# Another order of expert blocks and of their weight loads, and another place for the shared down products, in a two-layer transformer kernel

## The chip, the cores and the metric

The kernel runs on one core of a Trainium2 chip. The metric is the device time of one execution in microseconds (us); the median of several runs stands for a kernel. One more execution was profiled, and the rows below come from it.

The engines of the core have their own instruction streams and meet through semaphores. TensorE (PE in the rows) multiplies matrices into PSUM; its weight loads (PEld) run beside the products. VectorE (DVE) and ScalarE (ACT) work on tiles, GpSimd (POOL) here mostly gathers token rows, and SyncE (SP, or SPq for its queue) issues nearly all transfers from memory. Transfers that SyncE issues go out in its program order: when one has to wait for its buffer, all that stand behind it wait too.

## The reference, cut to what matters

One token sequence of 512 passes two blocks. The first has attention and then a mixture of experts, and that is where the change lies: 64 experts, 6 for each token, and a shared expert for all tokens.

```python
def moe_ffn(h, w_router, b_router, w_exp_gate, w_exp_up, w_exp_down, w_sh_gate, w_sh_up, w_sh_down):
    scores = jax.nn.sigmoid((xf @ w_router).astype(jnp.float32))
    ...
    def expert_block(xs):
        tok, g, e = xs
        xb = x_pad[tok]
        hb = jax.nn.silu(xb @ w_exp_gate[e]) * (xb @ w_exp_up[e])
        return (hb @ w_exp_down[e]) * g[:, None]
    ...
    routed = jax.ops.segment_sum(yb.reshape(n_rows, D), row_tok, num_segments=T + 1)[:T]
    shared = (jax.nn.silu(xf @ w_sh_gate) * (xf @ w_sh_up)) @ w_sh_down
    return (shared + routed).reshape(B, S, D)
```

The model width D is 1024 and an expert's inner width 256, all in float32. So an expert has a gate and an up matrix of 1024 x 256 and a down matrix of 256 x 1024, three MB in all.

## The kernel before

The work of the experts is cut into 32 blocks of 128 token slots. A block serves one, two or three experts: `KINDS` gives how many blocks there are of each kind and how the 128 slots are shared out. Two blocks are fixed to experts 0 to 3, 5 have one expert (128 slots), 5 have three (64, 32, 32), and the other 20 have two (96, 32 or 64, 64). Which expert falls to which place is found at run time, by how many tokens each has.

The list `seq` sets the order in which TensorE takes the blocks. For each block TensorE does, in program order: the gate and up products (`expert_h`, line 1009, on `raw`, `rawh`, `rawl` or `raws` weights), the transposes of the next block's tokens (line 994), the first half of the products that add the block before into the residual (`combine`, lines 1054 and 1055), the transpose of the hidden values (line 1019), the second half of `combine`, and the down products (`expert_out`, line 1033, on `whi`, `wlo` or `rawd` weights). After some blocks small products follow that work out the token slots of later blocks (`slot_info`, line 971).

The weights come by SyncE. A gate/up load is half of an expert's gate and up matrix, two transfers of 512 KB, and takes one place in a ring of buffers `gu` (3 `rawh`, 6 `raw`, 2 `rawl`, and, after the first round, the one buffer `raws`). A down load is half of a down matrix, one transfer of 512 KB, and takes one place in a ring of eight (3 `whi`, 3 `wlo`, 2 `rawd`). Before the loop, `phase_b` writes the list `stream` of all loads. Time is counted in half steps there: 2i is the gate/up of the i-th block of `seq`, 2i + 1 its down products. `free` is the half step that gives the load's buffer back. The list is sorted, and `issue(now)` takes loads from its head as long as their buffers are free at half step `now`.

The shared expert's down products are four chunks of 128 tokens, each of four 512-wide products that stand as two instructions each (line 1409, on `raws` and `hsT`). Their weights `wd` lie in the buffer `raws` from before the loop. `down_at` says after which block's gate/up a chunk comes: before, the chunks are in the blocks 0, 1, 2 and 3. `raws` joins the ring of `gu` when the fourth is done.

After the block before the last come a test for experts with more tokens than slots, the last block, and the second model block.

Of the kernel before, what the change touches and what calls it, by code (L numbers as in the profile page):

```python
# [17 lines left out]
OP = mybir.AluOpType  # L18
AX = mybir.AxisListType

T, D, NCH = 512, 1024, 4
# [37 lines left out]
class Kern:  # L59
# [861 lines left out]

    def gu(self, h):
        self.turn += 1
        n = self.NP + self.NX + self.NY
        t = self.turn if self.turn < n else (self.turn - n) % (n + 1)
        if t < self.NP:
            return self.hold.tile([128, self.RAW], F32, name="rawh", bufs=self.NP)
        if t < self.NP + self.NX:
            return self.raw(2048)
        return self.spare() if t < n else self.last()  # L930

    def last(self):
        return self.rp.tile([128, self.RAW], F32, name="raws")
# [124 lines left out]
    def phase_b(self):  # L1058
        nc, tc, I = self.nc, self.tc, self.I
        xr, hT, hp = self.xres, self.h2T, self.hp  # L1060
# [6 lines left out]
        wd = self.last().rearrange("p (k n) -> p k n", k=2)  # L1067
# [34 lines left out]
        hsT = rt.tile([128, 2, T], F32, name="hsT")  # L1102
# [11 lines left out]
        for j in range(3):  # L1114
            t = rt.tile([128, D], F32, name=f"xg{j}")
# [5 lines left out]
        p = 0  # L1121
# [75 lines left out]
        p = 0  # L1197
# [6 lines left out]
        for name, src in (("pos", pos), ("gate", sco)):  # L1204
            t = self.tps()
# [4 lines left out]
            t = self.tps()  # L1210
# [45 lines left out]
        def info(bs):  # L1256
            b0, b1 = bs[0], bs[-1] + 1
            return self.slot_info(ep, b1 - b0, [(x, y, slot[:, :, o * NB + b0:o * NB + b1], lambda c, j, o=o: pay[:, c, o * NB + b0 + j, :])
                                                for x, y, o in self.parts(b0)], (tok[:, b0:b1], tokf[:, b0:b1], gate[:, b0:b1]))
# [8 lines left out]
        ks = [list(range(p, p + n)) for p, n in zip(np.cumsum([0] + [k[0] for k in self.KINDS]).tolist(), [k[0] for k in self.KINDS])]  # L1268
        seq = ks[0][:]
        for i, p in enumerate(ks[2] + ks[3] + ks[5]):  # L1270
            seq.append(p)
            if i % 4 == 2:
                seq += [ks[4].pop(0), ks[1].pop(0)]
        assert sorted(seq) == list(range(NB))


# [1 line left out]
        n = 2  # L1278
        while todo:
            p = todo[0]  # L1280
# [4 lines left out]
            n = 3  # L1285

        stream, ngu, ndn = [], self.NP + self.NX + self.NY, self.NHI + self.NLO + self.ND
        ug, ud = [], []  # L1290
        for i, p in enumerate(seq):
            es = self.experts(p)
            for h in range(2):
                for j in es:
                    t = len(ug)
                    free = -1 if t < ngu else 2 * ug[t - ngu] if t < 2 * ngu else 7 if t == 2 * ngu else 2 * ug[t - ngu - 1]
                    ug.append(i)
                    if i >= STAT:
                        stream.append((free, 2 * i, len(stream), p, j, h))
            for j in es:  # L1300
                for k in range(2):
                    t = len(ud)
                    free = -1 if t < ndn else 2 * ud[t - ndn] + 1
                    ud.append(i)
                    if i >= STAT:
                        stream.append((free, 2 * i + 1, len(stream), p, j, 2 + k))
        last = {0: -1, 1: -1}
        for n, (free, *r) in enumerate(stream):
            last[r[-1] > 1] = free = max(free, last[r[-1] > 1])
            stream[n] = (free, *r)  # L1310
        stream.sort()
        ids_of = {}

        def issue(now):

            while stream and stream[0][0] <= now:
                _, _, _, p, j, h = stream.pop(0)
                if (p, j) not in ids_of:
                    ld, (e,) = nc.values_load_multi_w_load_instructions(
                        ids[0:1, j * NB + p:j * NB + p + 1], engines=[mybir.EngineType.SP], min_val=0, max_val=E - 1)  # L1320
                    if len(ends) > 2:
                        self.order(ends[-3], ld[0])
                    ids_of[p, j] = e
                e, w = ids_of[p, j], loads.setdefault(p, {}).setdefault(j, [None] * 4)
                if h < 2:
                    w[h] = self.load_gu(self.gu(h), dyn, e, h)
                else:
                    w[h] = self.load_down(self.down(h - 2), dyn, e, h - 2)
                    ends.append(self.last_load)

        down_at = {0: [0], 1: [1], 2: [2], 3: [3]}
        ends, done = [], []
        fixed_down(1, 1)
        issue(-1)
        for d in sorted(k for k in due if k < 0):
            for bs in due.pop(d):
# [38 lines left out]
        def up(xT, p):  # L1375
            parts = tiles(p)
            return parts, self.expert_h(parts, xT, gate[:, p:p + 1])
# [5 lines left out]
        for i, p in enumerate(seq):  # L1383
            infos = [info(bs) for bs in due.get(i, [])]
            for g in infos[:1]:
                next(g)
            if nxt is None:
                nxt = up(xT, p)
            (parts, hs), nxt = nxt, None
            if i == NB - 2:  # L1390
                self.combine(done)
                done = []
                self.chain = None
                overflow()
                self.chain = []
            issue(2 * i)
            if i + 3 < NB:
                q = seq[i + 3]
                self.gather(xgs[i % 3], tok[:, q:q + 1])
            if i + 1 < NB:  # L1400
                xT = self.slots_T(xgs[(i + 1) % 3])
                if i + 1 >= NB - 1:
                    nxt = up(xT, seq[i + 1])
            for c in down_at.get(i, []):
                for n in range(2):
                    pd = self.acc()
                    s = slice(n * 512, (n + 1) * 512)
                    for k in range(2):
                        self.pe(nc.tensor.matmul(pd, hsT[:, k, c * 128:(c + 1) * 128], wd[:, k, s], start=(k == 0), stop=(k == 1)))
                    nc.vector.tensor_tensor(xr[:, c, s], xr[:, c, s], pd, op=OP.add)  # L1410
            y = None
            if i == NB - 1:
                y = self.hold.tile([128, self.RAW], F32, name="rawh", bufs=self.NP).bitcast(F32R)
                y = Split(y[:, :D], y[:, D:])
            if done and i < NB - 1:
                self.combine(done, range(0, 2))
            hT = self.hidden_T(hs)
            if done and i < NB - 1:
                self.combine(done, range(2, NCH))
                done = []  # L1420
            done.append((self.pick(tokf[:, p:p + 1]), self.expert_out(parts, hT, y)))
            for g in infos:
                self.run(g)
            issue(2 * i + 1)
        self.chain = None
        assert not stream
# [687 lines left out]
```

## Time and profile before

| what | value |
|---|---|
| median of three timed runs | 1771.95 us (1765.51 to 1772.01) |
| the profiled execution's own time | 1765.15 us |
| its span, first to last instruction | 1763.4 us |
| TensorE busy in the span | 1690.5 us (96%) |
| VectorE, ScalarE, GpSimd busy | 976.9, 581.4 and 69.0 us |
| mean granted clock of TensorE | 0.985 of full speed |
| moved by transfers | 341.90 MB, 194 GB/s on the mean over the span |

The expert blocks take the time from about 504 to 1052 us of the span. "Busy" says that an instruction was under way, not that it ran at full speed. The rows count idle time of an engine only ahead of an instruction, with what ended it. The granted clock is a share of 2.4 GHz: 1.00 is that level, 0.50 the level of 1.2 GHz, and a number between them a mixture over the stretch.

### The profile page before, as it was taken

What the parts mean: (1) busy time and instruction counts of PE and PEld (TensorE: products, weight loads), DVE (VectorE), ACT (ScalarE), POOL (GpSimd) and SP (SyncE); (2) the same over time, 40 slices, a digit from 0 to 9 for tenths busy, and PEclk for the clock granted to TensorE, in tenths of its full rate; (3) what the DMA queues carried; (4) which work ended last, traced back from release to release, by engine and by line L of the source; (5) the groups of instructions that cost most, each with busy time, mean ns of one, the idle gap of its engine ahead of it and who ended that gap; (6) DMA issues with size and microseconds to landing.
All of it is one profiled execution on the core that took longest, in us unless ns stands there. A gap on an engine that the chain in (4) does not pass through costs nothing. (4 is left out here: it accounts for less than half of the span.)

```text
span 1763.4 us, 23536 instructions
## 1 busy us (share of the span) xinstructions
PE 1690.5 (96%) x8740; PEld 1130.1 (64%) x8743; DVE 976.9 (55%) x1910; ACT 581.4 (33%) x1112; POOL 69.0 (4%) x107
## 2 busy tenths in 40 slices
PE   7899999999899999899999988999998999999999
PEld 2677766787654444354535437767866788888887
DVE  5585656366846665456546548655455744224422
ACT  3565444423111111111111123454557443114311
POOL 0000000000310000000000010000000000000000
PEclk9999999999999999999999998999999999999999
DMA  9233426138768999999999933201200432233230
GB/s 306 79 121 97 135 96 209 46 114 322 292 264 307 387 408 406 403 403 403 403 396 400 376 135 94 91 19 60 73 24 25 144 96 96 96 96 96 96 119 24
DMA packets 137895, 341.90 MB, mean 194 GB/s; under 512 B 12986, under 2 KB 59389, under 8 KB 137775
## 3 DMA queue, kind: packets, MB, share of 16 engines
q1 hardware_dynamic: 133168, 327.76, 50.7%
q0 software_dynamic: 4608, 12.59, 1.9%
q8 instruction: 71, 1.16, 0.3%
q14 instruction: 48, 0.39, 0.1%
HBM read 340.26 MB, written 4.21 MB: 195 GB/s over the span
## 5 line engine op out<-in xcount | busy, mean ns | idle before, releaser
L89 DVE TENSOR_TENSOR wlo<-raw,whi 128x1024 fp32r<-128x1024 f32 (+4 forms) x162 | 189.6, 1172 | 251.2 <-ACT whi L88 249.6
L88 ACT ACTIVATE whi<-raw 128x1024 fp32r<-128x1024 f32 (+4 forms) x162 | 164.4, 1019 | 253.3 <-PE acc L123 159.9
L1056 DVE TENSOR_TENSOR xres<-xres,acc 128x512 f32<-128x512 f32 x248 | 151.3, 682 | 0.5 <-PE acc L1055 0.5
L1009 PE MATMUL acc<-raw,xT 128*32 128x512 f32 (+2 forms) x704 | 140.2, 602 | 0.0
L121 PE MATMUL acc<-m_hh,whi 128*128 128x512 f32 (+1 forms) x272 | 103.4, 382 | 2.0 <-ACT m_hh L88 2.0
L1054 PE MATMUL acc<-yh,S 128*128 128x512 f32 x248 | 104.5, 421 | 0.0
L123 PE MATMUL acc<-m_hh,wlo 128*128 128x512 f32 (+1 forms) x272 | 103.7, 382 | 0.0
L122 PE MATMUL acc<-m_hl,whi 128*128 128x512 f32 (+1 forms) x272 | 103.7, 382 | 0.0
L88 ACT ACTIVATE yh<-yg 128x512 fp32r<-128x512 f32 x62 | 39.1, 630 | 194.8 <-DVE yg L1035 194.8
L123 PE MATMUL acc<-whi,ul 128*128 128x512 f32 x256 | 101.1, 395 | 0.0
L122 PE MATMUL acc<-wlo,uh 128*128 128x512 f32 x256 | 101.1, 395 | 0.0
L121 PE MATMUL acc<-whi,uh 128*128 128x512 f32 x256 | 101.1, 395 | 0.0
L1033 PE MATMUL acc<-wlo,hT 128*32 128x512 f32 (+2 forms) x312 | 98.9, 642 | 1.1 <-ACT hT L1021 1.1
L1009 PEld LDWEIGHTS acc<-raw,xT 128*32 128x32 f32 (+2 forms) x704 | 48.8, 131 | 79.5 <-issue 72.2
L1012 DVE SCALAR_TENSOR_TENSOR hs<-hs,gate,acc 128x256 f32<-128x256 f32 x32 | 15.4, 480 | 150.1 <-ACT hs L1011 150.1
L1055 PE MATMUL acc<-yl,S 128*128 128x512 f32 x248 | 97.5, 393 | 0.0
L1033 PE MATMUL acc<-whi,hT 128*32 128x512 f32 (+2 forms) x256 | 76.2, 628 | 13.9 <-DMA whi<-in_w_exp_down_dram 12.8
L121 PE MATMUL acc<-hh,whi 128*128 128x512 f32 x192 | 80.9, 421 | 0.0
L123 PE MATMUL acc<-hh,wlo 128*128 128x512 f32 x192 | 76.9, 401 | 0.0
L122 PE MATMUL acc<-hl,whi 128*128 128x512 f32 x192 | 76.9, 400 | 0.0
L1011 ACT ACTIVATE hs<-acc 128x256 f32<-128x256 f32 x32 | 12.3, 384 | 176.8 <-PE acc L1009 176.8
L286 DVE TENSOR_REDUCE st<-s 128x1 f32<-128x128 f32 (+1 forms) x96 | 46.5, 486 | 36.2 <-PE s L324 20.5
(612 smaller groups left out, 3548.3 us busy)
## 6 DMA issues: line engine op xcount, KB each, us to landing
raw<-in_w_exp_gate_dram SPq DMA_DIRECT2D x66, 512.0 KB
raw<-in_w_exp_up_dram SPq DMA_DIRECT2D x66, 512.0 KB
whi<-in_w_exp_down_dram SPq DMA_DIRECT2D x48, 512.0 KB
wlo<-in_w_exp_down_dram SPq DMA_DIRECT2D x48, 512.0 KB
raw<-in_w_in_dram SPq DMA_DIRECT2D x21, 1024.0 KB
rawh<-in_w_exp_gate_dram SPq DMA_DIRECT2D x33, 512.0 KB
rawh<-in_w_exp_up_dram SPq DMA_DIRECT2D x33, 512.0 KB
raw<-in_w_mod_dram SPq DMA_DIRECT2D x16, 1024.0 KB
```

The costliest lines, as they stand in the source:

```text
L88: self.nc.scalar.activation(hi, src, AF.Copy)
L89: return self.nc.vector.tensor_tensor(lo, src, hi.bitcast(F32), op=OP.subtract)
L121: mm(out, lh, rh, start=start, stop=False)
L122: mm(out, lh, rl, start=False, stop=False)
L123: mm(out, ll, rh, start=False, stop=stop)
L286: nc.vector.tensor_reduce(st[:, 1:2], s_ps[:, :n], axis=AX.X, op=OP.max, negate=True)
L1009: self.pe(nc.tensor.matmul(pg[a:b].rearrange("p (u n) -> p u n", u=2), xT[:, kk, a:b], ws[kk // 4][:, kk % 4], start=(kk == 0), stop=(kk = ...
L1012: nc.vector.scalar_tensor_tensor(hs, hs, gate, pg[:, 256:], op0=OP.mult, op1=OP.mult)
L1033: self.pe(nc.tensor.matmul(p[a:b], hT[:, j, a:b], ws[2 + j][:, s], start=(j == 0), stop=(j == 1)))
L1054: self.pe(nc.tensor.matmul(p, l, y.hi[:, s], start=(i == 0), stop=False))
L1055: self.pe(nc.tensor.matmul(p, l, y.lo[:, s], start=False, stop=(i == len(done) - 1)))
L1056: nc.vector.tensor_tensor(xr[:, c, s], xr[:, c, s], p, op=OP.add)
```

## The change

Three things change in the code. First, `seq`: before, after the third, seventh, eleventh, fifteenth and nineteenth of the two-expert blocks come a block of three and then one of one; now, after the third, fifth, seventh, ninth and eleventh, a block of one and then one of three. Written with F for a fixed block, 1, 2 and 3 for blocks of one, two and three experts:

```
before  F F 2 2 2 3 1 2 2 2 2 3 1 2 2 2 2 3 1 2 2 2 2 3 1 2 2 2 2 3 1 2
after   F F 2 2 2 1 3 2 2 1 3 2 2 1 3 2 2 1 3 2 2 1 3 2 2 2 2 2 2 2 2 2
```

Second, `stream` is sorted by the half step at which a load is wanted less 4 (`2 * i - 4` for gate/up, `2 * i - 3` for down), or by `free` where that is later, and no longer by `free` alone. A load at the head still waits until its buffer is free, and the others behind it wait with it. Third, the four chunks of shared down products go into the first four blocks of three, behind `combine` and right ahead of the down products; the buffer `raws` stays with them until then and never joins the ring of `gu`, which has 11 places throughout.

```diff
--- before.py
+++ after.py
@@ -921,13 +921,12 @@
     def gu(self, h):
         self.turn += 1
-        n = self.NP + self.NX + self.NY
-        t = self.turn if self.turn < n else (self.turn - n) % (n + 1)
+        t = self.turn % (self.NP + self.NX + self.NY)
         if t < self.NP:
             return self.hold.tile([128, self.RAW], F32, name="rawh", bufs=self.NP)
         if t < self.NP + self.NX:
             return self.raw(2048)
-        return self.spare() if t < n else self.last()
+        return self.spare()
     def last(self):
         return self.rp.tile([128, self.RAW], F32, name="raws")
@@ -1269,8 +1268,8 @@
         seq = ks[0][:]
         for i, p in enumerate(ks[2] + ks[3] + ks[5]):
             seq.append(p)
-            if i % 4 == 2:
-                seq += [ks[4].pop(0), ks[1].pop(0)]
+            if i % 2 == 0 and 2 <= i <= 10:
+                seq += [ks[1].pop(0), ks[4].pop(0)]
         assert sorted(seq) == list(range(NB))
@@ -1286,6 +1285,7 @@
         stream, ngu, ndn = [], self.NP + self.NX + self.NY, self.NHI + self.NLO + self.ND
         ug, ud = [], []
         for i, p in enumerate(seq):
@@ -1293,28 +1293,28 @@
             for h in range(2):
                 for j in es:
                     t = len(ug)
-                    free = -1 if t < ngu else 2 * ug[t - ngu] if t < 2 * ngu else 7 if t == 2 * ngu else 2 * ug[t - ngu - 1]
+                    free = -1 if t < ngu else 2 * ug[t - ngu]
                     ug.append(i)
                     if i >= STAT:
-                        stream.append((free, 2 * i, len(stream), p, j, h))
+                        stream.append((max(free, 2 * i - 4), free, 2 * i, len(stream), p, j, h))
             for j in es:
                 for k in range(2):
                     t = len(ud)
                     free = -1 if t < ndn else 2 * ud[t - ndn] + 1
                     ud.append(i)
                     if i >= STAT:
-                        stream.append((free, 2 * i + 1, len(stream), p, j, 2 + k))
+                        stream.append((max(free, 2 * i - 3), free, 2 * i + 1, len(stream), p, j, 2 + k))
         last = {0: -1, 1: -1}
-        for n, (free, *r) in enumerate(stream):
-            last[r[-1] > 1] = free = max(free, last[r[-1] > 1])
-            stream[n] = (free, *r)
+        for n, (at, *r) in enumerate(stream):
+            last[r[-1] > 1] = at = max(at, last[r[-1] > 1])
+            stream[n] = (at, *r)
         stream.sort()
         ids_of = {}
         def issue(now):
-            while stream and stream[0][0] <= now:
-                _, _, _, p, j, h = stream.pop(0)
+            while stream and stream[0][1] <= now:
+                p, j, h = stream.pop(0)[-3:]
                 if (p, j) not in ids_of:
                     ld, (e,) = nc.values_load_multi_w_load_instructions(
                         ids[0:1, j * NB + p:j * NB + p + 1], engines=[mybir.EngineType.SP], min_val=0, max_val=E - 1)
@@ -1328,7 +1328,8 @@
                     w[h] = self.load_down(self.down(h - 2), dyn, e, h - 2)
                     ends.append(self.last_load)
-        down_at = {0: [0], 1: [1], 2: [2], 3: [3]}
+        down_at = {i: [c] for c, i in enumerate([i for i, p in enumerate(seq) if len(self.experts(p)) == 3][:NCH])}
         ends, done = [], []
         fixed_down(1, 1)
         issue(-1)
@@ -1401,13 +1402,6 @@
                 xT = self.slots_T(xgs[(i + 1) % 3])
                 if i + 1 >= NB - 1:
                     nxt = up(xT, seq[i + 1])
-            for c in down_at.get(i, []):
-                for n in range(2):
-                    pd = self.acc()
-                    s = slice(n * 512, (n + 1) * 512)
-                    for k in range(2):
-                        self.pe(nc.tensor.matmul(pd, hsT[:, k, c * 128:(c + 1) * 128], wd[:, k, s], start=(k == 0), stop=(k == 1)))
-                    nc.vector.tensor_tensor(xr[:, c, s], xr[:, c, s], pd, op=OP.add)
             y = None
             if i == NB - 1:
                 y = self.hold.tile([128, self.RAW], F32, name="rawh", bufs=self.NP).bitcast(F32R)
@@ -1418,6 +1412,13 @@
             if done and i < NB - 1:
                 self.combine(done, range(2, NCH))
                 done = []
+            for c in down_at.get(i, []):
+                for n in range(2):
+                    pd = self.acc()
+                    s = slice(n * 512, (n + 1) * 512)
+                    for k in range(2):
+                        self.pe(nc.tensor.matmul(pd, hsT[:, k, c * 128:(c + 1) * 128], wd[:, k, s], start=(k == 0), stop=(k == 1)))
+                    nc.vector.tensor_tensor(xr[:, c, s], xr[:, c, s], pd, op=OP.add)
             done.append((self.pick(tokf[:, p:p + 1]), self.expert_out(parts, hT, y)))
             for g in infos:
                 self.run(g)
```

On SyncE, around the loads of the first block of three (blocks 5 and 7 before; 6 and 7 now). The names carry buffer numbers here: `whi_5117` and `whi_5119` are the two down loads of its third expert before, the `raw` loads the gate/up of the block two places further on. Before:

```order
L954 DMA rawd_4946<-in_w_exp_down_dram 128x1024
...
L954 DMA rawd_4948<-in_w_exp_down_dram 128x1024
...
L950 DMA raw_5012<-in_w_exp_gate_dram 128x1024
...
L950 DMA raw_5025<-in_w_exp_gate_dram 128x1024
...
L950 DMA raw_5028<-in_w_exp_gate_dram 128x1024
...
L950 DMA raw_5031<-in_w_exp_gate_dram 128x1024
...
L954 DMA whi_5117<-in_w_exp_down_dram 128x1024
...
L954 DMA whi_5119<-in_w_exp_down_dram 128x1024
```

Now, with `rawd_4932` the first expert's first down load, `whi_5039` and the two rows behind it the rest, and `raw_5055` the first gate/up load of the next block:

```order
L953 DMA rawd_4932<-in_w_exp_down_dram 128x1024
...
L953 DMA rawd_4934<-in_w_exp_down_dram 128x1024
...
L953 DMA whi_5037<-in_w_exp_down_dram 128x1024
...
L953 DMA whi_5039<-in_w_exp_down_dram 128x1024
...
L953 DMA whi_5041<-in_w_exp_down_dram 128x1024
...
L953 DMA wlo_5043<-in_w_exp_down_dram 128x1024
...
L949 DMA raw_5055<-in_w_exp_gate_dram 128x1024
```

The six down loads of the block of three now stand together and ahead of the next block's gate/up loads; before, the last two stood behind four gate/up loads of a later block.

On TensorE, around the first chunk of shared down products. Before, in block 0, between the transposes for the next block and the hidden values' transpose (block 0 has nothing to combine):

```order
L994 MATMUL t<-ident,xg_3745 128x128 x8
L1409 MATMUL acc<-raws,hsT 128x512 x4
L1019 MATMUL ht<-ident,hs 128x128 x2
L1033 MATMUL acc<-whi,hT 32x512 x7
L1033 MATMUL acc<-wlo,hT 32x512
```

Now, in block 6, between the last products of `combine` (1053 and 1054 are the lines 1054 and 1055 of before) and the down products (line 1033 before):

```order
L1053 MATMUL acc<-yh,S 128x512
L1054 MATMUL acc<-yl,S 128x512
L1420 MATMUL acc<-raws,hsT 128x512 x4
L1032 MATMUL acc<-rawd,hT 32x512 x2
L1032 MATMUL acc<-whi,hT 32x512 x2
```

The chunk has left block 0 and stands in front of the down products of the first block of three.

## Rows read from the trace of the kernel before

**Rows 1.** The page: its head, and busy time (us, share, instructions).

```profile
span 1763.4 us, 23536 instructions
...
PE 1690.5 (96%) x8740; PEld 1130.1 (64%) x8743; DVE 976.9 (55%) x1910; ACT 581.4 (33%) x1112; POOL 69.0 (4%) x107
```

**Rows 2.** Timeline, PE, blocks 0 and 30: start us, us, instruction.

```profile
503.97 1.05 PE L1009 MATMUL acc<-rawh,xT 128*32 128x512 f32 x2 [0.33 <-ACT xT L999]
...
1016.31 7.13 PE L1009 MATMUL acc<-raw,xT 128*128 128x512 f32 x16
```

**Rows 3.** Windows: length, busy by engine, granted clock, DMA share, GB/s.

```profile
540.00:560.00 20.00, 20.00 (x170) 10.15 (x166) 12.68 (x26) 2.63 (x5) 0.99 (x1) 1.00 0.82 317
560.00:574.00 14.00, 14.00 (x111) 5.67 (x104) 7.17 (x18) 2.24 (x4) 1.98 (x2) 1.00 0.62 212
600.00:1000.00 400.00, 387.17 (x2134) 185.89 (x2130) 230.62 (x430) 62.50 (x119) 22.82 (x23) 0.98 1.02 403
900.00:1000.00 100.00, 96.36 (x474) 45.20 (x470) 54.51 (x96) 15.65 (x30) 4.96 (x5) 0.97 1.02 399
712.00:720.00 8.00, 6.59 (x27) 1.59 (x28) 1.59 (x3) 0.63 (x1) 0.00 (x0) 0.57 1.02 399
```

**Rows 4.** Timeline, PE, an undisturbed block of two experts and the next start.

```profile
766.99 3.60 PE L1009 MATMUL acc<-rawh,xT 128*64 128x512 f32 x16
770.42 3.60 PE L1009 MATMUL acc<-raw,xT 128*64 128x512 f32 x16
...
779.05 0.64 PE L1033 MATMUL acc<-wlo,hT 128*64 128x512 f32 x1
...
782.53 7.04 PE L1009 MATMUL acc<-raw,xT 128*64 128x512 f32 x32
```

**Rows 5.** DMA view, 503 to 1017 us: total, the gathers' queue (packets, MB).

```profile
DMA packets 55724, 199.53 MB, mean 388 GB/s; under 512 B 7108, under 2 KB 7108, under 8 KB 55681
...
q0 software_dynamic: 4320, 11.92, 6.1%
...
xg<-h2d,tok POOLq DMA_INDIRECT x30, 7.4
```

**Rows 6.** Waits of PE, 503 to 1017 us: total us, times, longest.

```profile
PE acc L1033 <- DMA whi<-in_w_exp_down_dram: 12.8, 5, 6.0
```

**Rows 7.** Timeline, PE, down products of the second block of three.

```profile
706.34 0.62 PE L1033 MATMUL acc<-wlo,hT 128*32 128x512 f32 x2
...
713.41 1.06 PE L1033 MATMUL acc<-whi,hT 128*32 128x512 f32 x1 [6.01 <-DMA whi<-in_w_exp_down_dram]
```

**Rows 8.** Windows of line 1033 alone, undisturbed and five times disturbed.

```profile
778.00:784.00 6.00, 3.65 (x16) 1.00 1.03 405
608.00:616.00 8.00, 4.89 (x32) 1.00 1.03 408
705.00:720.00 15.00, 7.40 (x32) 0.77 1.02 404
809.00:820.00 11.00, 6.50 (x32) 0.84 1.02 401
909.00:922.00 13.00, 7.18 (x32) 0.74 1.02 399
1010.00:1017.00 7.00, 4.68 (x32) 1.00 0.31 112
```

**Rows 9.** Timeline, PE, a chunk of the shared down products.

```profile
550.52 3.60 PE L1409 MATMUL acc<-raws,hsT 128*128 128x512 f32 x8
```

**Rows 10.** Timeline, SP's queue, around raws and a late down load.

```profile
562.53 0.33 SPq L954 DMA_DIRECT2D wlo<-in_w_exp_down_dram  x1
573.63 0.34 SPq L950 DMA_DIRECT2D raws<-in_w_exp_gate_dram  x1
...
690.46 0.33 SPq L950 DMA_DIRECT2D raw<-in_w_exp_gate_dram  x1
...
701.97 0.33 SPq L954 DMA_DIRECT2D whi<-in_w_exp_down_dram  x1
```

## The prediction

> **What bounds the kernel now.** I read the page first: a span of 1763.4 us with TensorE busy for 96% of it [rows 1]. That share hides what the change touches, so the next view is the stretches of the expert stage, from the first gate/up product of block 0 at 503.97 us to that of block 30 at 1016.31 us [rows 2]: 512.3 us. Read the last two columns of [rows 3]: from 600 to 1000 us the DMA engines run at a share of 1.02 and 403 GB/s, full all the time, but from 540 to 560 us they move 317 GB/s and from 560 to 574 us only 212. So inside one stage the transfers idle early and are the limit later.
>
> How near is TensorE to a limit of its own? One undisturbed block of two experts takes 782.53 - 766.99 = 15.54 us from gate/up to gate/up; its down products begin 12.06 us after its start and take 3.5 us [rows 4]. A two-expert block needs 12 transfers of 512 KB, 6.29 MB, plus its gathered tokens (a share of 11.92 MB over 30 gathers, 0.40 MB) [rows 5]: 6.69 MB / 403 GB/s = 16.6 us. The engine needs 15.5 us a block, the weights 16.6: nearly balanced, and slightly in favour of the engine waiting.
>
> Where it waits is in one place. The table of waits gives 12.8 us, five times, longest 6.0, for down products on a down weight [rows 6]. The timeline shows the longest: the products start at 706.34 us, stop, and resume at 713.41 us [rows 7]. And they resume slower: 1.06 us for a product that took 0.62 just before, the granted clock over 712 to 720 us being 0.57, a mixture of the 2.4 GHz level and the 1.2 GHz one, after the engine stood still for 6 us [rows 3, 7]. To price the slow part I compare the busy time of the down products in five stretches with an undisturbed one [rows 8]: 4.89 + 7.40 + 6.50 + 7.18 + 4.68 = 30.65 us against 5 x 3.65 = 18.25, so 12.4 us more. Waits and their slow aftermath cost 12.8 + 12.4 = **25.2 us**. All five are blocks of three experts. Without them the stage would take 512.3 - 25.2 = **487.1 us**. A cross-check: 30 x 15.54 = 466.2, plus four shared chunks of about 3.5 (3.60 with the pipeline's end) [rows 9] = 14.0, leaves 7 us for the slot products between blocks, which is plausible.
>
> **The change, part by part.**
>
> *Order of the loads.* Take the second block of three. Eight gate/up transfers of a block further on are issued from 690.46 us on, and only then, at 701.97 us, the third expert's down weights [rows 10]; two transfers later they are used at 713.41, some 10 us after their issue. They were wanted at 706.34. The new list puts all six down loads of a block of three ahead of the next block's gate/up. And with a block of one expert in front, the ring of eight makes the third expert's loads wait for down buffers of the block two places before, not, as now, of the block just before. That gives 15.5 us more, against a lateness of 7 at most (713.41 - 706.34). I cost the removal at -25.2 us, the whole of the waits, since the lead grows by more than twice the worst wait.
>
> *Shared down products.* 32 matmuls (4 chunks) leave blocks 0 to 3 and enter the first four blocks of three. TensorE's work is the same: 0 us by itself, as matmuls do not vanish. What moves is time: blocks 0 to 3 end 3.5 us sooner each, so buffers come free sooner while transfers have room (317 and 212 GB/s), and in a block of three the 3.5 us lie ahead of the down products and give the weights that much longer. On VectorE two additions a chunk go along; it is not full, 230.6 us busy of 400 [rows 3]. I take 0.
>
> *One buffer less.* The shared weights stay in the buffer "raws" until the fourth block of three, so the ring has 11 places, not 12. This also takes a wait off the load queue: after 562.53 us nothing is issued until 573.63 us, when the first load into "raws" goes, right when chunk 3 releases it; everything behind it waits for 11 us, and this is the 212 GB/s stretch [rows 3, 10]. Price: a twelfth of the read-ahead, about a quarter of a block (4 us of lead). That cover is spent where the transfers are full anyway; bound it between 0 and the lead, 4 us once. I take 0.
>
> *A new wait.* Ordering by need puts down loads, which wait for buffers, ahead of gate/up loads whose buffers are already free. Queued behind a waiting down load on SyncE are the gate/up loads of the next block, and TensorE waits for those. At the start it means that block 3's gate/up is issued only after block 0's down products. It is wanted two blocks later, 31 us, and some eight transfers of 1.3 us (0.524 MB / 403 GB/s) are ahead of it, 10 us: hidden. What the new order can cost is idle transfer time.
>
> *The ledger of transfers.* From 503 to 1017 us 199.53 MB moved [rows 5]. Not wanted before block 30's second half of gate/up are block 30's down weights and all of block 31, 16 transfers, 8.4 MB. The other 191.1 MB at 403 GB/s need 474 us: done at 503 + 474 = 977 us if never idle. TensorE would want the last at 504 + 487 + 3.5 = 994.5. So 17 us of idle transfer time may be lost before the weights, not TensorE, set the end. Before, the loss was 20 x (403 - 317)/403 = 4.3 and 14 x (403 - 212)/403 = 6.6 us, 11 together [rows 3]. I expect about 6 (the wait for raws is gone, the new wait comes), so a margin of 11. At the rate of the lowest 100 us, 399 GB/s [rows 3], 5 us of it go; at 390 GB/s, 16 us, and it is overdrawn by 5.
>
> A rule that speaks against the change is weighed here. The row says 403 GB/s, held for 400 us [rows 3]. The Trainium skill (DMA: Bandwidth & Descriptors, Specifications) gives a limit of about 358 GB/s from memory for one core; by it the same bytes would take 534 us, and the stage would be longer than now. The trace disagrees with that figure where one core is at work, and the sum goes by the row.
>
> *Sum.* The profiled execution took 1765.15 us, 1.75 more than its span [rows 1]. 1765.15 - 25.2 = 1740.0. I add 1 us for a small wait that I can't see: **1741 us**. The three timed runs had a median of 1771.95, 6.8 above the profiled one, which is near the fastest of them (1765.51); the changed kernel may have such a spread too, and the range takes it in.
>
> **The rivals.**
>
> 1. *Part of it comes back.* The block after each block of three gets its second expert's down weights only when the three-expert block has released theirs, 12.06 us before use. A load into a full queue took some 10 us [rows 10], and two are needed (1.3 each): about 12.6, late by 0.5, and by 2 or 3 where the queue runs as slowly as in those rows ((701.97 - 690.46) / 8 = 1.44 us a transfer, not 1.3); a long stop would add the slow clock, (7.40 + 7.18 - 7.30) / 2 = 3.6 us [rows 8]. Five times 2 to 3 is 10 to 15 lost: 1750 to 1756. Against it: the six gate/up transfers just in front can be issued when the three-expert block's gate/up products end, 8.5 us sooner, so that the queue need not be full.
>
> 2. *Transfers were the limit anyway.* If the new waits leave them idle for 42 us in place of 11, the margin of 17 is overdrawn by 25 and the waits only change places: 1765. For it: the balance of 15.5 to 16.6 us a block, and a list that holds ready loads behind waiting ones. Against it: the first four blocks turn over faster, and the 11 us of room lie there.
>
> 3. *Slower.* Same place as rival 1, one price higher: if those six gate/up transfers are held as well, by a down load in front that waits, the second expert's weights stand behind 6 + 8 transfers, 14 x 1.3 = 18, and land 9 us late with 3.6 us of slow clock: 12.6 x 5 = 63, less 25.2: 1803. It decides from 5.0 us lost per block of three.
>
> 4. *The sustained rate falls.* With TensorE never stopping, the transfers have no more time in which to catch up. The time stays as it is if 191.1 MB fill the 516.8 us from 503 to 1019.8 (block 30's start now, and 3.5): 370 GB/s; 5% less than that, 352, is 26 us slower, 1791. Against it: no full 100 us have less than 399 [rows 3]. The Trainium skill's figure named above would give 503 + 534 - 1019.8 = 17 us more, 1782.
>
> **How the numbers follow.** Forecast (waits gone, 1735 to 1747): 0.75. Rival 1 (to 1757): 0.15. Rival 2: 0.06. Rival 3: 0.03. Rival 4: 0.01. The range 1735 to 1757 us leaves out little over 1 in 10 of these, and holds 8 in 10 with the runs' own spread. Half a percent, 8.8 us, is about what a measurement of this kernel can tell from no change. Faster by more than that: 0.75 + 0.15 = 0.90; within it 0.06; slower 0.04.
>
> **What would show it.** In the changed profile the waits of down products on down weights should fall from 12.8 us to under 2, the clock over 600 to 1000 us should read 1.00 and not 0.98, the stretch from first gate/up to block 30's should be 485 to 490 us, blocks 0 to 3 should be 3.5 us shorter, and the transfers should run above 390 GB/s from about 520 us on. Wrong would be: a wait on down weights in the block after each block of three (rival 1 or 3), on gate/up weights near the end (rival 2), or the same stage length with transfers full from 520 us on.

## The result, and the profile after

The changed kernel takes 1744.73 us (median of 4 runs, 1743.85 to 1748.16) against 1771.38 us of the kernel before in the same measurement (4 runs, 1765.51 to 1772.01). The ratio is 0.986, with a 95% interval of 0.9836 to 0.9885. The forecast was 1741 us, in a range of 1735 to 1757. A second measurement of the same two kernels (e9 below, 6 and 11 runs) gave 1747.5 against 1767.44 us, a ratio of 0.9882 (0.9862 to 0.9902). So the gain is 26.7 us in one measurement and 19.9 in the other.

The profiled execution took 1743.85 us. Its page, the span and the busy time by engine:

```profile
span 1741.8 us, 23494 instructions
...
PE 1680.4 (96%) x8742; PEld 1128.4 (65%) x8743; DVE 976.6 (56%) x1910; ACT 580.9 (33%) x1112; POOL 68.9 (4%) x107
```

TensorE's share, 96%, is that of [rows 1]: it says nothing of the change. The timeline of TensorE does, at the first gate/up products of blocks 0, 4 and 30 (helpers' line numbers are one less than before):

```profile
503.78 1.04 PE L1008 MATMUL acc<-rawh,xT 128*32 128x512 f32 x2 [0.33 <-ACT xT L998]
...
567.07 1.90 PE L1008 MATMUL acc<-raw,xT 128*32 128x512 f32 x16
...
991.24 0.59 PE L1008 MATMUL acc<-rawl,xT 128*64 128x512 f32 x1
```

The stage is 991.24 - 503.78 = 487.5 us, against 512.3 in [rows 2]: 24.9 us shorter. The forecast had 487.1. Blocks 0 to 3 take 63.3 us together; before, block 4 starts at 581.78 us, so they took 77.8: 14.5 us, or 3.6 a block, have left them. They come back as the chunks in the blocks of three.

The table of TensorE's waits from 500 to 1000 us answers to [rows 6]. It holds two rows, neither of them on a transfer:

```profile
PE acc L1032 <- ACT hT L1020: 0.5, 1, 0.5
PE acc L1008 <- ACT xT L998: 0.3, 1, 0.3
```

The windows answer to [rows 3]; the third column from the end is the granted clock, then DMA share and GB/s:

```profile
504.00:520.00 16.00, 15.53 (x158) 6.93 (x160) 8.22 (x21) 2.62 (x5) 1.97 (x2) 1.00 0.92 351
520.00:540.00 20.00, 20.00 (x174) 9.12 (x170) 13.54 (x33) 2.63 (x5) 1.98 (x2) 1.00 0.98 386
540.00:560.00 20.00, 20.00 (x188) 10.46 (x181) 11.04 (x26) 3.60 (x7) 0.98 (x1) 1.00 1.02 408
560.00:574.00 14.00, 14.00 (x113) 5.60 (x112) 8.39 (x14) 1.64 (x3) 0.99 (x1) 1.00 0.80 302
600.00:1000.00 400.00, 400.00 (x2260) 191.25 (x2249) 238.78 (x442) 63.97 (x122) 21.75 (x22) 1.00 1.02 403
900.00:1000.00 100.00, 100.00 (x486) 47.63 (x483) 56.83 (x104) 16.12 (x31) 3.96 (x4) 1.00 1.02 405
```

From 600 to 1000 us TensorE is busy for all of the 400 us at a clock of 1.00 (before: 387.17 and 0.98), and the transfers keep their 403 GB/s beside it. The forecast of more than 390 GB/s from about 520 us on is missed in two stretches: 520 to 540 us with 386, and above all 560 to 574 us with 302. SyncE's queue says why for the second:

```profile
555.42 0.33 SPq L949 DMA_DIRECT2D rawl<-in_w_exp_up_dram  x1
566.44 1.19 SPq L953 DMA_DIRECT2D wlo<-in_w_exp_down_dram  x2
```

The wait of 11 us for `raws` [rows 10] is gone, but a wait as long stands in its place: a down load at the head of the list, whose buffer block 3 gives back with its down products. Nobody on TensorE waits for it here.

The span is only 21.6 us shorter, though the stage gained 24.9. Where the other 3.3 us went is the last group of experiments.

### The profile page after: what moved, and what is told of

Its sections match the earlier page's. It is cut to its first block, busy times and chain, and to the rows that moved or that the text cites. A ratio compares the mean times of both kernels' runs of the same rounds, so it can differ in the third digit from the quotient of the medians.

```text
span 1741.8 us, 23494 instructions
## 1 busy us (share of the span) xinstructions
PE 1680.4 (96%) x8742; PEld 1128.4 (65%) x8743; DVE 976.6 (56%) x1910; ACT 580.9 (33%) x1112; POOL 68.9 (4%) x107
## 5 line engine op out<-in xcount | busy, mean ns | idle before, releaser
L1008 PE MATMUL acc<-raw,xT 128*32 128x512 f32 (+2 forms) x760 | 146.6, 598 | 0.0
L1032 PE MATMUL acc<-wlo,hT 128*32 128x512 f32 (+2 forms) x272 | 91.1, 596 | 0.9 <-ACT hT L1020 0.9
L1008 PE MATMUL acc<-rawh,xT 128*32 128x512 f32 (+2 forms) x408 | 83.1, 594 | 0.3 <-ACT xT L998 0.3
L286 DVE TENSOR_REDUCE st<-s 128x1 f32<-128x128 f32 (+1 forms) x96 | 46.4, 485 | 36.3 <-PE s L324 20.5
```

The lines of the kernel that those rows point to most:

```text
L286: nc.vector.tensor_reduce(st[:, 1:2], s_ps[:, :n], axis=AX.X, op=OP.max, negate=True)
L1008: self.pe(nc.tensor.matmul(pg[a:b].rearrange("p (u n) -> p u n", u=2), xT[:, kk, a:b], ws[kk // 4][:, kk % 4], start=(kk == 0), stop=(kk = ...
L1032: self.pe(nc.tensor.matmul(p[a:b], hT[:, j, a:b], ws[2 + j][:, s], start=(j == 0), stop=(j == 1)))
```

## The experiments

**Theory A**: the gain comes from transfer time that is no longer lost in the first blocks (the wait for `raws`, and four chunks during which full buffers stop the transfers). **Theory B**: it comes from the order of blocks and loads alone, as the prediction's sum put it. Total times of one kernel spread by up to 13 us, and part of that arises behind the expert blocks, in work that the change doesn't touch: from block 30's start to the span's end the profiles of e1 and e2 take 758.0 and 751.1 us. So beside the totals (medians, with the ratio to runs of before on the same chip) I compare the stage (block 0's to block 30's first gate/up) in each profile. Each kernel of the table has one profile, but for the changed one, whose two (the second is e9's) give the same 487.5 us. A place is a block's number in `seq`, counted from 0. "Lost" is the transfer time lost from 504 to 600 us, (403 - GB/s) / 403 x 96.

| kernel | total, us | ratio to before (95%) | stage, us | GB/s 504 to 600 | lost, us | TensorE's wait on transfers, us |
|---|---|---|---|---|---|---|
| before (profiled) | 1765.15 | | 512.3 | 348 | 13.1 | 12.8 |
| sort of loads only | 1764.36 | 0.9981 (0.9965 to 0.9996) | 503.5 | 343 | 14.3 | 8.7 |
| order of blocks only | 1773.36 | 1.003 (1.0012 to 1.0047) | 514.1 | 320 | 19.8 | 17.4 |
| sort and block order | 1757.89 | 0.9948 (0.9927 to 0.9969) | 500.5 | 317 | 20.5 | 6.9 |
| ring of eleven only | 1759.75 | 0.9956 (0.9938 to 0.9975) | 503.3 | 371 | 7.6 | 9.5 |
| ring and chunks only | 1755.79 | 0.9923 (0.9895 to 0.9952) | 499.5 | 403 | 0 | 7.0 |
| after, old sort | 1754.39 | 0.9924 (0.9897 to 0.9952) | 493.0 | 406 | 0 | 2.6 |
| after, old chunks | 1757.94 | 0.9946 (0.9921 to 0.9971) | 501.1 | 322 | 19.3 | 7.4 |
| after, old block order | 1750.07 | 0.9889 (0.9859 to 0.9919) | 492.3 | 393 | 2.4 | 1.9 |
| after | 1744.73 | 0.986 (0.9836 to 0.9885) | 487.5 | 379 | 5.7 | 0 |

### One part alone

**e1, ring and chunks.** The kernel before with the chunks moved and, as they hold `raws` for longer, the ring of eleven; both orders as before. The chunk's own lines stand where the change puts them; the ring's other lines are those of e4.

```diff
-        down_at = {0: [0], 1: [1], 2: [2], 3: [3]}
+        down_at = {i: [c] for c, i in enumerate([i for i, p in enumerate(seq) if len(self.experts(p)) == 3][:NCH])}
...
-        return self.spare() if t < n else self.last()
+        return self.spare()
...
```

> The kernel before with one part of the change alone: the four shared down chunks in the first four blocks of three, and the buffer raws out of the ring of gate/up buffers (11 places). Order of blocks and order of loads as before. Theory A (the gain is transfer time that lay idle in the first four blocks): most of the gain, about 22 us, so a stage of 490 us from block 0's gate/up to block 30's, with a wait left at the last block of three only. Theory B (the gain comes from the order in which down weights are issued, on which the prediction's sum put all of it): the late down loads of the third expert stay late, under 5 us gained, stage above 507 us.

The stage came to 499.5 us, 12.9 gained: between the two. The window of the first blocks and the waits:

```profile
504.00:600.00 96.00, 95.53 (x819) 45.66 (x822) 59.70 (x127) 14.52 (x28) 6.92 (x7) 1.00 1.02 403
```

```profile
PE acc L1032 <- DMA whi<-in_w_exp_down_dram: 7.0, 8, 1.8
```

Not a microsecond of transfer time is lost any more, and still TensorE waits, eight times, for the third expert's down weights in blocks of three. So A holds for half of the gain; for the other half full transfers are not enough, and what they bring first matters.

**e2, sort of the loads.** Only the sort by need.

```diff
-                        stream.append((free, 2 * i, len(stream), p, j, h))
+                        stream.append((max(free, 2 * i - 4), free, 2 * i, len(stream), p, j, h))
...
```

> The kernel before with one part alone: the loads sorted by need. Blocks, shared chunks and the ring of 12 as before. Theory A: the first four blocks keep their length and about 8 us of transfer time still lie idle, so about 14 us gained, with waits of 2 to 5 us left at the later blocks of three; stage about 498 us. Theory B: 20 us or more, no waits on down weights.

The stage gained 8.8 us, short of both. Waits remain in the blocks of three from place 17 on, 6.9 us on `whi`, and a new one appears, on gate/up:

```profile
PE acc L1033 <- DMA whi<-in_w_exp_down_dram: 6.9, 5, 3.0
PE acc L1009 <- DMA rawh<-in_w_exp_up_dram: 1.8, 1, 1.8
```

**e3, order of the blocks.** Only `seq`.

```diff
-            if i % 4 == 2:
-                seq += [ks[4].pop(0), ks[1].pop(0)]
+            if i % 2 == 0 and 2 <= i <= 10:
+                seq += [ks[1].pop(0), ks[4].pop(0)]
```

> The kernel before with one part alone: the order of blocks, one ahead of three. Loads sorted by the time their buffer is free, shared chunks and ring of 12 as before. Theory A: about 5 us gained; waits move from the blocks of three to the blocks right behind them. Theory B: with the sort by need missing, 8 to 15 us, since the ring gives the third expert's down loads a block more.

Both theories had a gain; the stage lost 1.8 us. SyncE's queue, which stood still for 10.8 us behind 562 us in the kernel before, now stands there for 18.0. The waits left the blocks of three and stand in the block right behind each, on its second expert's down weights:

```profile
649.93 1.06 PE L1033 MATMUL acc<-rawd,hT 128*32 128x512 f32 x1 [7.85 <-DMA rawd<-in_w_exp_down_dram]
```

```profile
PE acc L1033 <- DMA rawd<-in_w_exp_down_dram: 17.4, 9, 7.8
```

That is the prediction's rival 1, place and all, where the block order is changed alone.

**e4, ring of eleven.** `raws` never joins the ring; the chunks stay in blocks 0 to 3.

```diff
-        t = self.turn if self.turn < n else (self.turn - n) % (n + 1)
+        t = self.turn % (self.NP + self.NX + self.NY)
...
```

> The kernel before with nothing changed but that the buffer raws never joins the ring (11 places): no load waits for the fourth shared chunk any more. Chunks stay in blocks 0 to 3. Theory A: the 11 us in which the load queue stood still are used, about 13 us gained, stage about 500 us, although there is a buffer less. Theory B: a buffer less is a little loss, 0 to 4 us slower.

The stage gained 9.0 us, less than A's and against B's sign. One buffer less makes the kernel faster: the load queue no longer stands still for the buffer that chunk 3 gives back, and the time lost falls from 13.1 to 7.6 us. The waits that remain, 9.5 us, are all in the last three blocks of three.

### One part taken back

**e5, old sort.** After, with the loads sorted by `free`.

```diff
-                        stream.append((max(free, 2 * i - 4), free, 2 * i, len(stream), p, j, h))
+                        stream.append((free, 2 * i, len(stream), p, j, h))
...
```

> The changed kernel with the loads sorted by the place at which their buffer comes free, as before the change; new block order, chunks in the blocks of three and ring of eleven stay. Theory A (what counts is that the transfers are never stopped in the first blocks and have room there; each part gives some of the same lead, so the last one adds little): the stage from block 0 to block 30 stays at 487 to 489 us, no wait on a transfer over 2 us, total 1742 to 1748. Theory B (each part is worth what it gave alone, and the sort gave 8.8 us of 24.9 there): stage 495 to 498, with waits of TensorE on down halves of 6 to 9 us in sum, total 1752 to 1756.

493.0 us: neither. (The total, 1754.39 us, is in B's range; but the profiled execution was the fastest of four, at 1749.45, and what the slower ones lost is in no profile.) The transfers are full from the start (406 GB/s), and one block still waits, at place 23. It stands behind the fifth block of three, the only one without a chunk:

```profile
896.43 0.64 PE L1032 MATMUL acc<-rawd,hT 128*64 128x512 f32 x1 [2.23 <-DMA rawd<-in_w_exp_down_dram]
```

```profile
893.00:903.00 10.00, 6.64 (x16) 1.54 (x16) 0.83 1.00 390
```

The second fence is the window of line 1032 alone there: 6.64 us busy for products that take 3.65 undisturbed [rows 8], at a granted clock of 0.83. A wait of 2.6 us in all cost 2.6 + 3.0 = 5.6 us, which is the whole loss of 5.5.

**e6, old chunks.** After, with the chunks back in blocks 0 to 3.

```diff
-        down_at = {i: [c] for c, i in enumerate([i for i, p in enumerate(seq) if len(self.experts(p)) == 3][:NCH])}
+        down_at = {0: [0], 1: [1], 2: [2], 3: [3]}
```

> The changed kernel with the four chunks of the shared down products back in blocks 0 to 3; block order, sort and ring of eleven stay. Theory A (a chunk of 3.5 us is time of TensorE in which a transfer can catch up, and it is worth most in the blocks of three, which take more bytes than their compute lasts): stage 495 to 502 us, waits on down halves in the blocks right behind the blocks of three, 1 to 4 us each and 8 to 12 in sum; total 1752 to 1758. Theory B, as the prediction had it (the place of the chunks moves no time by itself): stage 487 to 490, no wait over 2 us, total 1743 to 1748.

501.1 us, as A had it. 13.6 us of the gain go, more than with either order: "no time by itself" is refuted. The waits are where A put them, in blocks behind blocks of three (places 11, 19, 23), a little less than its 8 to 12:

```profile
PE acc L1032 <- DMA rawd<-in_w_exp_down_dram: 7.4, 4, 3.9
```

**e8, old block order.** After, with the old `seq`.

```diff
-            if i % 2 == 0 and 2 <= i <= 10:
-                seq += [ks[1].pop(0), ks[4].pop(0)]
+            if i % 4 == 2:
+                seq += [ks[4].pop(0), ks[1].pop(0)]
```

> The changed kernel with the old order of blocks (the block of three ahead of the block of one); sort, ring of eleven and chunks in the blocks of three stay. Theory A (the order of blocks adds little once the other parts have given the lead): stage 488 to 491 us, at most one or two waits, in the last blocks of three, 1 to 3 us in sum; total 1744 to 1749. Theory B (the prediction's first step: the block of one ahead is what ends the waits): stage 496 or more, waits in at least three of the five blocks of three, 8 us or more in sum; total 1753 or more.

492.3 us, 1.3 above A's bound and 3.7 below B's. The only waits are in the last block of three, again the one without a chunk:

```profile
PE acc L1032 <- DMA whi<-in_w_exp_down_dram: 1.9, 2, 1.7
```

### The prediction's first step by itself

**e11, sort and block order.** The two edits of e2 and e3 together, chunks and ring as before.

> The kernel before with both orders changed (blocks and loads), and the four chunks and the ring of twelve as before: the prediction's first step by itself. Theory B, as the prediction had it (this step ends all waits, 25.2 us): stage 487 to 490 us, waits on down halves under 2 us, total 1741 to 1747. Theory A (the orders are worth about half, since transfer time is still lost in blocks 0 to 3): stage 499 to 504 us, 330 GB/s or less over 504 to 600 us, waits of 6 to 10 us in blocks right behind the blocks of three, total 1756 to 1761.

500.5 us, as A had it: the first step is worth 11.8 us, not 25.2. With e1's 12.9 that makes 24.7 of the 24.9. Inside these halves what a part is worth depends on the others: the ring of eleven gains 9.0 us in the kernel before (e4) and nothing beside both new orders (500.5 us here, 501.1 in e6); the chunks' move gains 3.8 us beside the old orders (e4 to e1) and 13.6 beside the new ones (e6 to after).

The first blocks lose more transfer time than ever, and SyncE's queue shows the pattern. A gap stands four times, 10.6, 11.3, 10.2 and 14.3 us long, from 511, 530, 551 and 567 us on. The third of them:

```profile
504.00:600.00 96.00, 95.19 (x732) 44.97 (x731) 57.42 (x121) 13.74 (x26) 6.94 (x7) 1.00 0.83 317
```

```profile
550.65 0.33 SPq L950 DMA_DIRECT2D raw<-in_w_exp_up_dram  x1
561.14 1.48 SPq L954 DMA_DIRECT2D whi<-in_w_exp_down_dram  x3
```

```profile
PE acc L1033 <- DMA rawd<-in_w_exp_down_dram: 6.9, 7, 1.7
```

At the gap a down load stands at the head of the list and waits for down products. A chunk in that block lies in front of them and holds the release back by its 3.6 us [rows 9]. e6 and the changed kernel, which differ in nothing but the chunks' place, have the same four gaps: 10.2, 11.2, 9.2 and 14.8 us in e6, 7.3, 7.9, 5.6 and 10.7 in the changed kernel, 2.9 to 4.1 us less each time. The last of them in e6 (that of the changed kernel, from 555.42 to 566.44 us, stands in the section on the result):

```profile
563.46 0.46 SPq L949 DMA_DIRECT2D rawl<-in_w_exp_up_dram  x1
578.70 1.19 SPq L953 DMA_DIRECT2D wlo<-in_w_exp_down_dram  x2
```

That is how the parts hang together: the sort makes the queue wait for down products, and moving the chunks brings those products forward.

### The 3.3 us that were given back

Two losses can be located, of 2.1 and 1.5 us; the rest is made up of small shifts both ways. The first is at the test for experts with too many tokens, behind block 30's gate/up. In the profile after, TensorE's idle time ahead of the next transposes is 6.28 us (4.16 in the kernel before), and TensorE's queue stands in the test's branch for 5492 ns. SyncE comes to the same branch at 1004.0 us, straight from its last two loads. (The fences are the timeline of TensorE, that of SyncE's queue, and line 1346 by engine: count, duration in ns, start.)

```profile
1008.67 1.95 PE L993 MATMUL t<-ident,xg 128*128 128x128 f32 x8 [6.28 <-PEq L1346]
```

```profile
1001.83 2.06 SPq L953 DMA_DIRECT2D rawd<-in_w_exp_down_dram  x2
```

```profile
L1346 PEldq COMPARE_BRANCH  x1: 5492/5492/5492, 1002.6 to 1002.6; - x1
L1346 DVEq COMPARE_BRANCH  x1: 72/72/72, 1003.4 to 1003.4; - x1
L1346 SPq COMPARE_BRANCH  x1: 58/58/58, 1004.0 to 1004.0; - x1
```

In the kernel before, SyncE was there 10 us ahead of TensorE, and the branch took 3332 ns:

```profile
1031.71 0.67 PE L994 MATMUL t<-ident,xg 128*128 128x128 f32 x2 [4.16 <-DVE S L1042]
```

```profile
L1345 SPq COMPARE_BRANCH  x1: 58/58/58, 1017.1 to 1017.1; - x1
...
L1345 PEldq COMPARE_BRANCH  x1: 3332/3332/3332, 1027.7 to 1027.7; - x1
```

**e7, e9 and e10, the last loads held back.** After, with the last block's four down loads issued behind the test (e7, and again as e10 beside the changed kernel itself, e9).

```diff
         stream.sort()
+        stream[-4:] = [(at, 2 * NB - 4, *r) for at, _, *r in stream[-4:]]
```

> The changed kernel with the last four down loads (those of the last block) held back until behind the overflow test of block 30. Theory A (in the changed kernel the load queue is still paced by transfers when the engines come to that test, and the test waits for it): TensorE's idle time ahead of the transposes behind the test falls from 6.3 to about 4.2 us, block 30 to block 31 from 19.3 to about 17.3, and the total by about 2 us, to 1742 to 1743; the stage to block 30 stays at 487 to 488. Theory B (the test waits for something else): idle time 6 us or more, total the same within 1 us. Theory C (the four loads now come too late for the last block): the down products of the last block wait 2 us or more on their transfers, total the same or up to 3 us longer.

> The changed kernel as it is, timed beside the one with the last four down loads held back. Both theories: about 1744 us, stage 487 to 488, idle time ahead of the transposes behind the overflow test 6.3 us.

> The changed kernel with the last four down loads held back until behind the overflow test, beside the changed kernel as it is. Theory A (the two microseconds given back at the test are gained for good): 1.5 to 2.5 us less than the changed kernel, idle time at the test 4.2 us. Theory B (the gain is lost again later, in the second model block): the same within 0.7 us, though the idle time at the test is 4.2 us.

```profile
1006.04 1.95 PE L993 MATMUL t<-ident,xg 128*128 128x128 f32 x8 [4.24 <-PEq L1347]
```

```profile
1006.44 1.22 SPq L953 DMA_DIRECT2D wlo<-in_w_exp_down_dram  x2
```

```profile
L1347 SPq COMPARE_BRANCH  x1: 58/58/58, 998.2 to 998.2; - x1
...
L1347 PEldq COMPARE_BRANCH  x1: 3452/3452/3452, 1002.0 to 1002.0; - x1
```

In these fences (the same three views of e7) what theory A forecast came true: the idle time is 4.24 us and the branch 3452 ns; block 30 to block 31 takes 17.3 us and not 19.3; the stage is 487.4, and the last block doesn't wait for a transfer. So holding the loads back is worth 2 us at the test. e7 took 1742.4 us (ratio to before 0.9847, 0.9825 to 0.987). Beside each other, e10 took 1743.47 us (4 runs, 1742.63 to 1745.49) and e9 1747.5 (6 runs, 1741.18 to 1749.97); in those profiles block 30 to 31 takes 17.30 and 19.78 us. The profiles show the 2 us plainly; the medians differ by more, and e9's spread of 9 us doesn't let the totals alone show them. The kernel with the loads held back is the fastest version here.

Why the loads cost these 2 us is not shown. That TensorE waits for SyncE to arrive, as theory A has it, fits badly: VectorE comes to the branch 0.6 us ahead of SyncE and takes 72 ns, and TensorE's time does not follow SyncE's delay (5492 ns where SyncE came 1.4 us behind TensorE, 5952 in e9 and 5372 in e11 where it came 0.9 us behind). A rival fits all profiles: the branch takes TensorE longer while transfers run. In the four profiles in which it took 4989 ns or more (after, e6, e9, e11) they moved 343 to 384 GB/s during it, and in the other nine, with 3332 to 3732 ns, 135 or less. The windows of the branch, after and in e7:

```profile
1002.60:1008.10 5.50, 0.00 (x0) 0.00 (x0) 1.40 (x3) 0.00 (x0) 0.00 (x0) 0.73 0.98 384
```

```profile
1002.00:1005.50 3.50, 0.00 (x0) 0.00 (x0) 1.41 (x3) 0.00 (x0) 0.00 (x0) 0.84 0.35 135
```

Holding the loads back takes both away, SyncE's delay and the transfers, so no run here separates them.

The second loss is in the second model block. At 1383.38 us the same products are 23.4 us ahead of before (1406.82), at 1387.49 us 21.9 (1409.43), at the span's end 21.6. The profile after has a stretch at a lower granted clock there, which the profile before has not. Ahead of these products TensorE stood idle for the same 2.00 us in both:

```profile
1383.38 1.16 PE L121 MATMUL acc<-m_hh,whi 128*128 128x256 f32 x4 [2.00 <-ACT m_hh L88]
```

```profile
1406.82 0.96 PE L121 MATMUL acc<-m_hh,whi 128*128 128x256 f32 x4 [2.00 <-ACT m_hh L88]
```

The windows, after and then before:

```profile
1376.00:1396.00 20.00, 17.30 (x107) 15.42 (x107) 13.37 (x38) 6.70 (x10) 0.00 (x0) 0.91 0.20 60
```

```profile
1399.40:1419.40 20.00, 17.36 (x115) 15.16 (x114) 13.47 (x39) 7.30 (x11) 0.00 (x0) 1.00 0.25 76
```

All experiments' profiles have such a stretch there (ten microseconds at 0.83), and another some 60 us earlier; e1 and e4 with both orders as before are among them, and e2 and e3 with ring and chunks as before. So no part of the change decides it; whether other executions of the kernel before have it too, its one profile can't say, and the cause stays open.

## Why the prediction was right, and where its steps were not

**What bounds the kernel**: right. Waits and their aftermath were priced at 25.2 us and all went; the stage gained 24.9. The down products of a block of three now take 3.64 us, as the prediction's undisturbed row had it:

```profile
613.00:620.00 7.00, 3.64 (x32) 1.00 1.01 397
```

The slow clock, estimated at 3.6 us for a long stop, measured 3.0 in e5 behind a short one. Not all of the 12.4 us were slow clock, though: two of the five stretches of [rows 8] read a granted clock of 1.00, and their 4.89 + 4.68 - 2 x 3.65 = 2.3 us are something else.

**Order of the loads, -25.2 us**: this step failed. It gave the whole gain to the two orders, because the third expert's loads came late in the list. The runs show 11.8 us for both orders (e11), 8.8 of it from the sort alone, while the block order alone costs 1.8 (e3). By this split the order in which the loads stood was half of the cause; the other half is that the list as a whole ran behind. The step's argument on the blocks, that one block more of lead makes the third expert's loads come in time, failed by itself in e3: there the wait moved one block on.

**Shared down products, 0**, and **one buffer less, 0**: failed, and by the same amount the other way. Together they gain 12.9 us (e1), the ring alone 9.0 (e4, though nothing beside the new orders); with the rest in place, the chunks' move is worth 13.6 (e6). The prediction named both mechanisms, the blocks 3.5 us shorter while transfers have room and the load queue freed from `raws`, and then booked nothing, since matmuls "do not vanish" and a buffer less is less lead. It should have priced the transfer time they free. The two errors cancelled, and that is luck in part: the sum was right because its size came from the waits, and every cause it left out worked on those same waits.

**A new wait, hidden**: right only with the chunks moved. After has it, from 555.42 to 566.44 us, and no engine waits. With the chunks left in blocks 0 to 3 (e11, e6) it loses some 20 us of transfer time and TensorE waits for 7.

**The ledger of transfers**: its expected loss of about 6 us was 5.7, inside the margin of 17; e6 and e11, with 19.3 and 20.5 lost, overdraw it and wait again. But a kept ledger isn't enough, as e1 shows: nothing lost, and 12 us worse than after.

**The sum, 1741**: the profiled run took 1743.85. The 2.9 us more are in the main the 2.1 at the test, which the prediction did not look at (it went with block 30's start as the end of the stage), and the 1.5 at a lower clock in the second model block, less the 1 us set aside; the stage itself gave 0.3 less than forecast.

**Rival 1** is a real mechanism: it decides e3, and in e6 and e11 it is what remains. In after it doesn't show. e6, without the chunks in the blocks of three, has it behind three of them; e5, without the sort, has it behind the one block of three that holds no chunk. So chunks and sort both bear on the lead of the block behind. **Rival 4**: the rate held at 403 GB/s without TensorE's pauses. The figure of 358 GB/s that the prediction weighed from the Trainium skill is not the one for a core alone; the Trainium skill (HBM Reference, Specifications (TRN2)) says that a core streaming alone measures well above its share, and the 403 GB/s here agree.

## What to carry to other kernels

A table of waits gives the size of a gain, not its cause: when several edits meet at one wait, run each alone and each taken back before believing the one that stands nearest to it. Where transfers are the limit late and idle early, what delays a buffer's release in the early blocks, be it compute that could stand elsewhere or a buffer that holds up the whole in-order queue, costs as much as a bad order of loads. And a loop's end is worth a look of its own: here a test cost TensorE 2 us more when the last loads ran into it.

## What the runs showed of the hardware

A branch on a value that all engines test took TensorE's queue 3332 to 3732 ns in nine profiles and 4989 to 5952 ns in the four in which transfers ran at 343 GB/s or more meanwhile, SyncE having just come from its last loads; VectorE's and SyncE's own queues took 72 and 58 ns each time. What holds TensorE there was not taken apart. The Trainium skill (Runtime: NRT & Kernel Launch, Instruction fetch mechanics) says that a taken branch can stall on fetching its target; no run here separates that.

The granted clock behind a short wait is not settled by the wait in these rows. In e5 the down products behind a wait of 2.23 us read 0.83. In the second model block the same products stand behind an idle time of 2.00 us in both kernels, and only one profile reads 0.91 around them, the other 1.00.
